# A hybrid decoder block on one Trainium2 core: sums of w_out's blocks made in DRAM by accumulating transfers instead of on GpSimd

## The chip, the core and the metric

The kernel runs on one core of a Trainium2 chip, as one program. The metric is device microseconds from one execution of the program; a time without further words is the median of several runs. The profile is one execution of its own, taken by the hardware profiler, with times in microseconds from the start of its span.

## The reference, cut to what matters

One decoder block on 1024 tokens of width 1024, with 16 meta tokens in front of them, so 1040 rows. All is float32.

```python
h = rmsnorm(x, norm_g)                       # 1040 x 1024
proj = h @ w_in                              # u_pool, z_pool, q, k, v, z_attn, f_logit, g_pool, g_attn
y_pool = causal_multiscale_pool(u_pool, pool_w, pool_scale) * silu(z_pool)
y_attn = forgetting_attention(q, k, v, log_f) * silu(z_attn)      # 8 heads of 64, causal
merged = sigmoid(g_pool) * (y_pool @ w_up_pool) + sigmoid(g_attn) * (y_attn @ w_up_attn)
out = rmsnorm(x + merged @ w_out, final_norm_g)   # w_out: 1024 x 1024
```

## The kernel before, in words

Every large product is made of three matmuls on high and low parts: an operand is rounded to float32r on ScalarE (the high part), and VectorE or GpSimd subtracts that from the operand (the low part).

The program has five stages. In the **first** (0 to about 56 us) the rows are read in nine tiles `xt` of 128 tokens (the ninth has 16). Of each tile ScalarE sums the squares (L184), VectorE adds the epsilon (L113), GpSimd raises to the power -0.5 (L114, `rstd`, through the helper `rstd_of`), VectorE scales the tile (L189), TensorE transposes it (L210, and L197 for the ninth tile), and ScalarE and VectorE make its high part `hh` (L212, L201) and low part `hl` (L213, L202). The list `todo` (L431 to L433) interleaves this with the projections of the first head pair: four token ranges times q, k and v. In the text the nine tiles are counted 0 to 8.

In the **second** stage (to about 503 us) the attention runs over 16 units (4 head pairs, 2 heads, 2 halves of the queries), in the loop at L682; the free time of TensorE is filled with the other projections, whose results are spilled to DRAM. In the **third** (to about 659 us) the pooling branch, the gates and the two up-projections follow, in the order of the list `steps`. The result `merged`, transposed, lies in eight tiles `G`; its four blocks of 512 by 512 are named "11" to "22" by `side`. The **fourth** (to about 736 us) is the product with `w_out` by seven products of blocks instead of eight (a Strassen-Winograd scheme): `prep` splits the operands of a product into high and low parts (`split_op`), `prod` runs 48 matmuls for each four output tiles, and `plus` and `arrive` add the results to the rows of x in `xr`. The **fifth** is the final norm and the stores.

The seven products need sums of blocks on both sides. On the side of `G` they are made by `s_first`, `s_second` and `s_third`. On the side of `w_out` they are made, in place in SBUF, by `t_first`, `t_second` and the second half of `s_third`, all on GpSimd, in pieces of 128x256, between 591 and 693 us. `w_load` brings `w_out` in as eight tiles `W` of 128 rows of 4 KB, one for each of eight up-projection steps.

What sets the order: TensorE's instructions run in the order in which the program is written. Those of the other engines, and the DMA issues of their queues (SP's above all), are put in order when the program is built, by a list scheduler that takes instructions as soon as it holds them to be ready, unless an `after` or `behind` ties them; each engine then runs its list in that order. The call `sums_of_w(i)` of the changed kernel stands in the loop over attention units, but its place in the code ties it to nothing.

Of the kernel before, what the change touches and what calls it, by code (L numbers as in the profile page):

```python
# [43 lines left out]
def r32(ap):  # L44
    return ap.bitcast(F32)
# [7 lines left out]
def tile_hybrid_block(ctx, tc, x, meta, norm_g, w_in, b_forget, pool_w, pool_scale,  # L53
                      w_up_pool, w_up_attn, w_out, final_g, out):
    nc = tc.nc
# [5 lines left out]
    wout = w_out[0].rearrange("(k p) n -> p k n", p=128)  # L61
# [6 lines left out]
    gp = ctx.enter_context(tc.tile_pool(name="gp", bufs=13))  # L68
    stg = ctx.enter_context(tc.tile_pool(name="stg", bufs=2))
    sm = ctx.enter_context(tc.tile_pool(name="sm", bufs=2))  # L70
    dr = ctx.enter_context(tc.tile_pool(name="dr", bufs=1, space=bass.MemoryType.DRAM))
# [28 lines left out]
    def after(ins, prev):  # L100
        tc.add_manual_dep(ins.ins, prev.ins.name,
                          mybir.DependencyInfo(mybir.DependencyClass.NoSync, mybir.DependencyReason.DATA),
                          reason="order")

    def behind(ins, prev):
        tc.add_manual_dep(ins.ins, prev.ins.name,
                          mybir.DependencyInfo(mybir.DependencyClass.Sync, mybir.DependencyReason.DATA),
                          reason="wait")
# [13 lines left out]
    def pool_tt(out, x, y, op):  # L122
        for c in range(0, out.shape[-1], 256):
            ins = nc.gpsimd.tensor_tensor(out[:, c:c + 256], x[:, c:c + 256], y[:, c:c + 256], op=op)  # L124
        return ins
# [142 lines left out]
    def v_piece(p, w, t0, t1):  # L268
        ps = yield from g_proj(w, t0, t1)
        nc.scalar.activation(VT[p][:, t0:t1], ps, AF.Copy)  # L270
# [59 lines left out]
    class Fill:  # L330
        def __init__(self):
            self.must, self.free, self.debt, self.now, self.cur, self.last = [], [], 0.0, 0, None, None
# [71 lines left out]
    def split_lo(raw, hi, pool, tag):  # L404
        lo = pool.tile([128, KO, 128], F32R, name="wlo", tag=tag)
        nc.gpsimd.tensor_tensor(lo, raw, r32(hi), op=ALU.subtract)
        return hi, lo
# [19 lines left out]
    wk = split_lo(rk, hk_, wp, "wl")  # L427
# [6 lines left out]
    for n, (kind, t0, t1) in enumerate(todo):  # L434
# [6 lines left out]
        else:  # L441
            g = v_piece(0, wv, t0, t1)
# [5 lines left out]
        i = {0: 2, 1: 3, 3: 4, 4: 5, 6: 6, 7: 7}.get(n)  # L448
# [7 lines left out]
        i = {1: 4, 2: 5, 4: 6, 5: 7, 6: 8}.get(n)  # L456
# [77 lines left out]
    for p in range(4):  # L534
        spill["y", p] = dr.tile([128, SEQ], F32, name=f"sp_y{p}")

    class Unit:
        def __init__(self, p, e, half):
            self.p, self.e, self.half = p, e, half
# [109 lines left out]
    def merged(a, c):  # L649
        out_ = []  # L650
        for lst in (a, c):
            tot = sum(s[0] for s in lst) or 1
            acc = 0.0
            for s in lst:
                out_.append(((acc + 0.5 * s[0]) / tot, s))
                acc += s[0]
        for _, (w, dve, pe, f) in sorted(out_, key=lambda t: t[0]):
            f()
            F.pull(max(0.0, PACE * dve - pe))
# [22 lines left out]
    for i, u in enumerate(units):  # L682
        nxt = units[i + 1] if i + 1 < 16 else None
        F.now = i
        if nxt is not None and nxt.p != u.p:
            F.until(f"q{nxt.p}", f"k{nxt.p}")
        merged(list(nxt.a_steps()) if nxt else [], list(u.c_steps()))
        for b in range(u.nb - LAG, u.nb):
            F.pull(LATENCY)
            u.av(b)  # L690
        if i == 1:
            after(nc.scalar.activation(pwh, pw, AF.Copy), exps[-1])
            nc.gpsimd.tensor_tensor(pwl, pw, r32(pwh), op=ALU.subtract)
        if nxt is not None:
            nxt.maxes()
        u.finish()
        if nxt is not None and nxt.p != u.p:
            F.until(f"v{nxt.p}")
            pair_fill(nxt.p + 1)
# [107 lines left out]
    G, gt, ya, muls = {}, {}, [], []  # L807
# [81 lines left out]
    hq = ctx.enter_context(tc.tile_pool(name="hq", bufs=8, side="right", reuse_waits="tile"))  # L889
# [4 lines left out]

    W = {}
    T_ = (slice(0, 512), slice(512, 1024))

    def w_load(k):
        W[k] = hq.tile([128, D], F32, name="W", tag="w")
        after(nc.sync.dma_start(W[k], wout[:, k, :]), muls[-1])  # L900

    def tt(out, x, y, op, eng):
        if eng is nc.gpsimd:
            pool_tt(out, x, y, op)
        else:
            eng.tensor_tensor(out, x, y, op=op)
# [5 lines left out]
    def pick(op_, k, n):  # L912
        return op_[n][k // 2][:, k % 2, :]

    def split_op(op_, k, src):
        h_ = pick(op_, k, 0)
        nc.scalar.activation(h_, src, AF.Copy)
        return nc.vector.tensor_tensor(pick(op_, k, 1), src, r32(h_), op=ALU.subtract)

    X3 = [gp.tile([128, 2, 512], F32, name="X3", tag="g") for _ in range(2)]  # L920
    Y3 = [gp.tile([128, 2, 512], F32, name="Y3", tag="g") for _ in range(2)]

    def side(d, k, blk):
        r, c = {"11": (0, 0), "12": (0, 1), "21": (1, 0), "22": (1, 1)}[blk]
        return d[k + 4 * r][:, T_[c]] if d is W else d[k + 4 * c][:, T_[r]]

    def t_first(k):
        tt(Y3[k // 2][:, k % 2, :], side(W, k, "22"), side(W, k, "12"), ALU.subtract, nc.gpsimd)
        tt(side(W, k, "12"), side(W, k, "12"), side(W, k, "11"), ALU.subtract, nc.gpsimd)

    def t_second(k):
        tt(side(W, k, "11"), side(W, k, "22"), side(W, k, "12"), ALU.subtract, nc.gpsimd)

    def s_first(k):
        tt(X3[k // 2][:, k % 2, :], side(G, k, "11"), side(G, k, "21"), ALU.subtract, nc.gpsimd)

    def s_second(k):
        tt(side(G, k, "21"), side(G, k, "21"), side(G, k, "22"), ALU.add, nc.vector)
        tt(side(G, k, "11"), side(G, k, "21"), side(G, k, "11"), ALU.subtract, nc.vector)

    def s_third(k, prev):
        for c in range(0, 512, 256):
            g12, g11 = [side(G, k, b)[:, c:c + 256] for b in ("12", "11")]
            ins = nc.gpsimd.tensor_tensor(g12, g12, g11, op=ALU.subtract)
            behind(ins, prev)
            w21, w11 = [side(W, k, b)[:, c:c + 256] for b in ("21", "11")]
            behind(nc.gpsimd.tensor_tensor(w21, w21, w11, op=ALU.subtract), prev)

    steps = [(0, 0), (1, 0), (2, 0), (3, 0), (0, 1)]
    for j in range(1, 8):  # L950
# [1 line left out]
    for n, s in enumerate(steps):  # L952
        for m, fn, d in ((n + 1, up_weights, ws), (n + 2, gate_row, rows_)):
            if m < len(steps) and steps[m] not in d:
                d[steps[m]] = fn(*steps[m])
        nxt = ws[steps[n + 1]][2] if n + 1 < len(steps) else None
        up(*s, ws.pop(s), rows_.pop(s), nxt)
        if n == 0:
            for p in range(4):
                attn_out(p)  # L960
        if 2 <= n < 10:
            w_load((0, 4, 1, 5, 2, 6, 3, 7)[n - 2])
            if n % 2:
                t_first((n - 2) // 2)
        j, a = s
        if a and j < 4:
            s_first(j)
        if s == (7, 0):
            opA, opB = operand("y"), operand("y")
        if a and j >= 4:  # L970
            if j < 6:
                for k in (2 * j - 8, 2 * j - 7):
                    split_op(opA, k, side(G, k, "11"))
                    split_op(opB, k, side(W, k, "11"))
                    t_second(k)
            if j == 5:
                s_second(0)
            if 4 < j < 7:
                s_second(j - 4)
# [18 lines left out]

    def plus(r, c0, ps):
        part = xr[r][:, c0:c0 + ps.shape[-1]]  # L1000
        return part, nc.vector.tensor_tensor(part, ps, part, op=ALU.add)

    def gain(r, c0, c1, eng):
        tt(xr[r][:, c0:c1], xr[r][:, c0:c1], fgb[:, c0:c1], ALU.mult, eng)
# [26 lines left out]
        after(nc.scalar.activation(o[:, b0:b1], xr[r][:, b0:b1], AF.Copy, scale=t), marks[-1][1])  # L1031
        nc.scalar.dma_start(o2[rr, b0:b1], o[:, b0:b1])

    srcs = [("11", "11"), ("12", "21"), ("11", "11"), ("21", "12"), (None, None), ("12", "22"), ("22", "21")]
    ops, lows = {0: (opA, opB)}, {}

    def prep(n):
        A_, B_ = operand("yh"[n % 2]), operand("yh"[n % 2])
        sa, sb = srcs[n]
        if n == 2:  # L1040
            s_second(3)
        for k in range(4):
            split_op(A_, k, side(G, k, sa) if sa else X3[k // 2][:, k % 2, :])
            lows[n] = split_op(B_, k, side(W, k, sb) if sb else Y3[k // 2][:, k % 2, :])
            if n == 3:
                s_third(k, lows[2])
        ops[n] = A_, B_

    lo_, hi_ = HALVES[0][0], HALVES[1][0]
    for n in range(7):  # L1050
        if n < 6:
            prep(n + 1)
        ps = ba if n in (0, 2, 4, 6) else bb_
# [56 lines left out]
```

## Time and profile before

| | |
|---|---|
| median of 3 runs | 744.41 us (744.18 to 745.41) |
| the profiled execution's own time | 743.96 us |
| its span | 742.2 us, so 1.76 us lie around the span |
| TensorE busy | 731.2 us, 99% |
| VectorE, ScalarE, GpSimd busy | 533.2, 377.0, 332.8 us |
| bytes moved by DMA | 75.35 MB |

A row of the timeline has the start, the duration, the engine, the line of the kernel, the operation, its output and inputs, a count where rows are merged, and in brackets how long the engine sat idle before it and whose event ended that. SPq is the queue on which SyncE issues transfers. A row of the windows has the stretch, its length, then for PE (TensorE), PEld (its weight load), DVE (VectorE), ACT (ScalarE) and POOL (GpSimd) the busy time and count, then TensorE's granted clock, the busy share of the DMA engines and GB/s. A row of the DMA table has the transfer, its queue, the count, the size of one and the median time from issue to landing.

### The profile page before, as it was taken

The page shows a single profiled execution, that of the slowest core. Times are in us where ns is not written, and L with a number is a line of the kernel's source. Part 1 is how long each engine was busy: PE and PEld are TensorE (multiplying, and loading weights), DVE is VectorE, ACT ScalarE, POOL GpSimd, SP SyncE. Part 2 cuts the span into 40 slices and gives each one's busy share as a digit, 9 for nine tenths or more (in the row PEclk, how much of TensorE's full clock was granted, in tenths as well). Part 3 has the DMA queues.
Part 4 walks back from the last instruction along what each step waited for, and adds up shares of the span by engine and source line. Part 5 has one row for each costly group of instructions (what it writes and reads, how often), then busy time and mean ns, then how long its engine had stood idle before and what let it go on. Part 6 is the DMA issues. An engine that isn't in the chain of part 4 may idle for free.

```text
span 742.2 us, 10619 instructions
## 1 busy us (share of the span) xinstructions
PE 731.2 (99%) x3686; PEld 622.7 (84%) x3686; DVE 533.2 (72%) x991; ACT 377.0 (51%) x736; POOL 332.8 (45%) x390
## 2 busy tenths in 40 slices
PE   8999999999999999999999999999999999999996
PEld 5997999988888898889988888888887888888885
DVE  5653577668779877688797687686288554997975
ACT  6662556446557545556563564452545322526445
POOL 4331235456426446345355383183348043606743
PEclk9999999999999999999999999999999999999998
DMA  9301132231312212222323223229375357360006
GB/s 301 88 15 43 29 86 86 62 98 23 95 48 60 80 50 90 78 53 55 94 66 86 80 80 92 72 81 309 95 201 212 142 200 240 116 224 1 1 0 227
DMA packets 76424, 75.35 MB, mean 102 GB/s; under 512 B 9665, under 2 KB 60865, under 8 KB 76370
## 3 DMA queue, kind: packets, MB, share of 16 engines
q1 hardware_dynamic: 74496, 69.95, 30.8%
q10 hardware_dynamic: 1874, 4.72, 1.7%
q8 instruction: 29, 0.48, 0.3%
q14 instruction: 25, 0.20, 0.1%
HBM read 55.58 MB, written 19.07 MB: 101 GB/s over the span
## 4 chain that ended last, share of the span: by engine, by line
PE 87%; DVE 5%; ACT 1%; issue 1%; POOLq 0%; POOL 0%; ACTq 0%
PE pj L152 65%; PE pj L995 8%; PE po L633 5%; PE ps L573 2%; PE ps L572 2%; PE pt L995 2%; PE pj L486 1%; DVE S L612 1%; DVE pl L617 1%; DVE ka L266 0%; PE pj L279 0%; DVE pt L603 0%; ACT S L581 0%; DVE mt L593 0%; ACT whi L140 0%
## 5 line engine op out<-in xcount | busy, mean ns | idle before, releaser
L124 POOL TENSOR_TENSOR wlo<-raw,whi 128x256 fp32r<-128x256 f32 x148 | 121.7, 852 | 192.5 <-ACT whi L140 96.1
L152 PE MATMUL pj<-hh,whi 128*128 128x512 f32 (+4 forms) x768 | 178.4, 360 | 0.6 <-ACT hh L201 0.3
L152 PE MATMUL pj<-hl,whi 128*128 128x512 f32 (+4 forms) x768 | 177.1, 359 | 0.0
L152 PE MATMUL pj<-hh,wlo 128*128 128x512 f32 (+4 forms) x768 | 174.4, 358 | 0.0
L152 PEld LDWEIGHTS pj<-hh,wlo 128*128 128x128 f32 x768 | 132.3, 188 | 18.1
L152 PEld LDWEIGHTS pj<-hh,whi 128*128 128x128 f32 x768 | 131.5, 188 | 18.7 <-ACT hh L201 0.5
L152 PEld LDWEIGHTS pj<-hl,whi 128*128 128x128 f32 x768 | 131.6, 188 | 17.7
L617 DVE TENSOR_TENSOR pl<-S,ph 128x512 fp32r<-128x512 f32 (+4 forms) x112 | 87.1, 792 | 19.3 <-ACT ph L616 18.8
L625 POOL TENSOR_TENSOR acc<-acc,S 128x272 f32<-128x272 f32 (+4 forms) x80 | 76.7, 958 | 11.2 <-ACT S L613 6.0
L581 ACT ACTIVATE S<-ps,negc 128x400 f32<-128x400 f32 (+2 forms) x96 | 49.3, 515 | 44.0 <-DVE S L579 35.7
L613 ACT ACTIVATE S<-S 128x512 f32<-128x512 f32 (+4 forms) x112 | 49.5, 478 | 33.7 <-DVE S L612 33.5
L616 ACT ACTIVATE ph<-S 128x512 fp32r<-128x512 f32 (+4 forms) x112 | 52.2, 480 | 15.8 <-PE po L633 14.4
L588 DVE TENSOR_TENSOR m<-m,S 128x272 f32<-128x272 f32 (+4 forms) x80 | 41.3, 517 | 23.8 <-ACT S L581 22.0
L140 ACT ACTIVATE whi<-raw 128x1024 fp32r<-128x1024 f32 x37 | 39.1, 1056 | 32.2 <-PE pj L152 27.8
L612 DVE TENSOR_TENSOR S<-S,pt 128x512 f32<-128x512 f32 (+4 forms) x112 | 51.9, 498 | 0.8
L836 DVE TENSOR_TENSOR rl<-pj,rl 128x512 f32<-128x512 f32 x32 | 22.0, 689 | 28.0 <-PE pj L152 28.0
L579 DVE SCALAR_TENSOR_TENSOR S<-ps,negc,mask 128x128 f32<-128x128 f32 (+2 forms) x72 | 23.7, 330 | 22.5 <-PE ps L573 22.3
L317 ACT ACTIVATE st<-pj 128x512 f32<-128x512 f32 x40 | 23.7, 593 | 28.1 <-PE pj L152 18.6
L633 PE MATMUL po<-pl,V 128*128 128x512 f32 (+4 forms) x112 | 37.6, 336 | 0.1
L573 PE MATMUL ps<-ql,ka 128*128 128x512 f32 (+4 forms) x112 | 37.5, 334 | 0.0
L572 PE MATMUL ps<-qa,ka 128*128 128x512 f32 (+4 forms) x112 | 36.0, 322 | 0.6 <-ACT S L581 0.5
L995 PE MATMUL pj<-opy 128*128 128x512 f32 (+1 forms) x168 | 36.3, 375 | 0.0
(187 smaller groups left out, 1134.2 us busy)
## 6 DMA issues: line engine op xcount, KB each, us to landing
raw<-in_w_in_dram SPq DMA_DIRECT2D x40, 512.0 KB, 3.9
sp_gp<-st SPq DMA_DIRECT2D x16, 256.0 KB, 2.0
sp_ga<-st SPq DMA_DIRECT2D x16, 256.0 KB, 2.0
rl<-sp_gp SPq DMA_DIRECT2D x8, 512.0 KB, 5.2
rl<-sp_ga SPq DMA_DIRECT2D x8, 512.0 KB, 4.5
W<-in_w_out_dram SPq DMA_DIRECT2D x8, 512.0 KB, 4.8
xr<-in_x_dram SPq DMA_DIRECT2D x8, 512.0 KB, 4.1
xt<-in_x_dram SPq DMA_DIRECT2D x7, 512.0 KB, 8.1
```

Source lines behind the costliest of these rows:

```text
L124: ins = nc.gpsimd.tensor_tensor(out[:, c:c + 256], x[:, c:c + 256], y[:, c:c + 256], op=op)
L152: nc.tensor.matmul(ps, a, b, start=(i == 0), stop=(i == len(seq) - 1))
L572: nc.tensor.matmul(ps[:kb, c0:], ka[:, k0:k0 + kb], qa[:, q0 + c0:q0 + 512], start=True, stop=False)
L573: nc.tensor.matmul(ps[:kb, c0:], ka[:, k0:k0 + kb], ql[:, q0 + c0:q0 + 512], start=False, stop=True)
L581: nc.scalar.activation(s[:kb, f0:], ps[:kb, f0:], AF.Identity, bias=nb_)
L612: nc.vector.tensor_tensor(s[:kb, c0:], s[:kb, c0:], self.pm[:kb, c0:], op=ALU.subtract)
L613: exps.append(nc.scalar.activation(s[:kb, c0:], s[:kb, c0:], AF.Exp))
L616: nc.scalar.activation(ph[:kb, c0:], s[:kb, c0:], AF.Copy)
L617: dves.append(nc.vector.tensor_tensor(pl[:kb, c0:], s[:kb, c0:], r32(ph[:kb, c0:]), op=ALU.subtract))
L625: nc.gpsimd.tensor_tensor(acc[:kb, c0:], acc[:kb, c0:], s[:kb, c0:], op=ALU.add)
L633: nc.tensor.matmul(self.po[:, c0:], v, r[:kb, c0:], start=(b == 0 and i == 0), stop=(b == self.nb - 1 and i == 1))
L995: nc.tensor.matmul(ps, pick(A_, k, p)[:, i * 128:(i + 1) * 128], pick(B_, k, q)[:, c0:c1], start=start and n == 0, stop=n == 11, skip_grou ...
```

## The change

The sums on the side of `w_out` are no longer made on GpSimd in SBUF. Four DRAM tensors of 512x512 (1 MB each) hold them: TD1 = W11 + W12, TD3 = W12 + W22, TD2 = TD3 + W11, TD4 = TD2 + W21. Each is first a plain copy (SP's queue), and then a transfer from GpSimd's queue adds a block of `w_out` to it at its destination (`accum_op`). The signs of the scheme are chosen anew so that all four are plain sums: the products that land in the right half are subtracted in `plus`, `split_op` makes a negated operand for product 2, and two combinations on the side of `G` change their sign. `w_load` now loads half a product's block (128x2x512, 512 KB) from `w_out` or from a TD; there are 14 of these loads instead of 8, and the last six are issued from `prep`. `t_first`, `t_second`, `Y3` and half of `s_third` are gone.

```diff
+    TD = {n: dr.tile([512, 512], F32, name=f"td{n}") for n in (1, 2, 3, 4)}
+    WB = {"11": w_out[0][:512, :512], "12": w_out[0][:512, 512:], "21": w_out[0][512:, :512], "22": w_out[0][512:, 512:]}
+
+    def sums_of_w(i):
+        if i == 2:
+            nc.sync.dma_start(TD[1], WB["11"])
+            nc.sync.dma_start(TD[3], WB["12"])
+        elif i == 4:
+            nc.gpsimd.dma_start(TD[1], WB["12"], accum_op=ALU.add)
+        elif i == 5:
+            nc.gpsimd.dma_start(TD[3], WB["22"], accum_op=ALU.add)
+        elif i == 7:
+            nc.sync.dma_start(TD[2], TD[3])
+        elif i == 8:
+            nc.gpsimd.dma_start(TD[2], WB["11"], accum_op=ALU.add)
+        elif i == 10:
+            nc.sync.dma_start(TD[4], TD[2])
+        elif i == 11:
+            nc.gpsimd.dma_start(TD[4], WB["21"], accum_op=ALU.add)
...
         u.finish()
+        sums_of_w(i)
...
-    def w_load(k):
-        W[k] = hq.tile([128, D], F32, name="W", tag="w")
-        after(nc.sync.dma_start(W[k], wout[:, k, :]), muls[-1])
+    WSRC = [WB["11"], WB["21"], TD[2], TD[1], TD[3], WB["22"], TD[4]]
+
+    def w_load(n, h):
+        W[n, h] = hq.tile([128, 2, 512], F32, name="W", tag="w")
+        return nc.sync.dma_start(W[n, h], WSRC[n].rearrange("(k p) c -> p k c", p=128)[:, 2 * h:2 * h + 2])
...
-    def split_op(op_, k, src):
+    def split_op(op_, k, src, neg=False):
         h_ = pick(op_, k, 0)
+        if neg:
+            nc.scalar.activation(h_, src, AF.Copy, scale=-1.0)
+            return nc.vector.scalar_tensor_tensor(pick(op_, k, 1), src, -1.0, r32(h_), op0=ALU.mult, op1=ALU.subtract)
...
-    def t_first(k):
-        tt(Y3[k // 2][:, k % 2, :], side(W, k, "22"), side(W, k, "12"), ALU.subtract, nc.gpsimd)
-        tt(side(W, k, "12"), side(W, k, "12"), side(W, k, "11"), ALU.subtract, nc.gpsimd)
-
-    def t_second(k):
-        tt(side(W, k, "11"), side(W, k, "22"), side(W, k, "12"), ALU.subtract, nc.gpsimd)
...
     def s_third(k, prev):
         for c in range(0, 512, 256):
             g12, g11 = [side(G, k, b)[:, c:c + 256] for b in ("12", "11")]
-            ins = nc.gpsimd.tensor_tensor(g12, g12, g11, op=ALU.subtract)
-            behind(ins, prev)
-            w21, w11 = [side(W, k, b)[:, c:c + 256] for b in ("21", "11")]
-            behind(nc.gpsimd.tensor_tensor(w21, w21, w11, op=ALU.subtract), prev)
+            behind(nc.gpsimd.tensor_tensor(g12, g11, g12, op=ALU.subtract), prev)
...
-        if 2 <= n < 10:
-            w_load((0, 4, 1, 5, 2, 6, 3, 7)[n - 2])
-            if n % 2:
-                t_first((n - 2) // 2)
+        if 4 <= n < 12:
+            after(w_load((n - 4) // 2, n % 2), muls[-1])
...
-        return part, nc.vector.tensor_tensor(part, ps, part, op=ALU.add)
+        if c0 < 512:
+            return part, nc.vector.tensor_tensor(part, ps, part, op=ALU.add)
+        return part, nc.vector.tensor_tensor(part, part, ps, op=ALU.subtract)
...
         ops[n] = A_, B_
+        if n < 4:
+            for h in range(2):
+                w_load(n + 3, h)
```

The change is a few lines of code, but it puts eight DMA issues into the lists of two queues. First stands GpSimd's list in the first stage of the kernel before, from the split of the first v weights on; `rstd` is the power of one tile, `ql` and `tri` are constants, and DMAHW and DMASW (in the next lists) are completions of transfers issued by SP or ScalarE, and by GpSimd.

```order
L406 TENSOR_TENSOR wlo<-raw,whi 128x1024 [waits DMAHW0_49,Activation_49]
L114 TENSOR_TENSOR rstd<-rstd,epsp 128x1 [waits DVE_49,Pool_49]
L480 MEMSET tri 128x256
L481 AFFINE_SELECT tri<-tri 128x128 [waits Pool_49]
L114 TENSOR_TENSOR rstd<-rstd,epsp 128x1 [waits DVE_49]
L223 MEMSET ql 64x1024 [waits Pool_49]
L223 MEMSET ql 64x1024
L114 TENSOR_TENSOR rstd<-rstd,epsp 128x1 [waits DVE_49,Pool_49]
L114 TENSOR_TENSOR rstd<-rstd,epsp 128x1 [waits DVE_49]
L114 TENSOR_TENSOR rstd<-rstd,epsp 16x1 [waits DVE_49]
```

In the changed kernel the same piece of GpSimd's list reads as follows, up to the last `rstd`. The names td_762, td_763, td_764 and td_765 are TD1, TD2, TD3 and TD4.

```order
L545 DMA td_762<-in_w_out_dram 512x512 [waits DMAHW4_49]
L114 TENSOR_TENSOR rstd<-rstd,epsp 128x1 [waits DVE_49,Pool_49]
L547 DMA td_764<-in_w_out_dram 512x512 [waits DMAHW5_49]
L480 MEMSET tri 128x256
L481 AFFINE_SELECT tri<-tri 128x128 [waits Pool_49]
L114 TENSOR_TENSOR rstd<-rstd,epsp 128x1 [waits DVE_49]
L223 MEMSET ql 64x1024 [waits Pool_49]
L223 MEMSET ql 64x1024
L551 DMA td_763<-in_w_out_dram 512x512 [waits DMAHW6_49]
L114 TENSOR_TENSOR rstd<-rstd,epsp 128x1 [waits DVE_49,Pool_49]
L555 DMA td_765<-in_w_out_dram 512x512 [waits DMAHW7_49]
L114 TENSOR_TENSOR rstd<-rstd,epsp 128x1 [waits DVE_49]
```

All four accumulating transfers have moved from the attention loop, where they are written, to among the `rstd` of tiles 4 to 8: one ahead of tile 4's, one ahead of tile 5's, one ahead of tile 6's, one ahead of those of tiles 7 and 8.

On SP's list the four plain copies stand behind the last small loads of the first stage (`psc`) and ahead of the weight loads of the second head pair (`raw`, L136). Before, the `raw` loads followed `psc` directly.

```order
L474 DMA psc<-in_pool_scale_dram 128x4x1 [waits DMAHW3_49]
L542 DMA td_762<-in_w_out_dram 512x512 [waits DMAHW4_49]
L543 DMA td_764<-in_w_out_dram 512x512 [waits DMAHW5_49]
L549 DMA td_763<-td_764 16x16384 [waits DMAHW6_49,DMASW1_49]
L553 DMA td_765<-td_763 16x16384 [waits DMAHW7_49,DMASW2_49]
L136 DMA raw<-in_w_in_dram 128x8x128 [waits DMAHW0_49,Activation_49,Pool_49]
```

The first two copies wait for nothing of the change; the third waits for the sum into TD3 (DMASW1), the fourth for the sum into TD2 (DMASW2). TensorE's list is the same in both kernels, and the lists of VectorE and ScalarE differ only in the stage of the seven products.

More of the change, by code (lines that the diff above doesn't have):

```diff
@@ L896, in tile_hybrid_block, with wk @@
     T_ = (slice(0, 512), slice(512, 1024))
-    def w_load(k):
-        W[k] = hq.tile([128, D], F32, name="W", tag="w")
-        after(nc.sync.dma_start(W[k], wout[:, k, :]), muls[-1])
+    WSRC = [WB["11"], WB["21"], TD[2], TD[1], TD[3], WB["22"], TD[4]]
+    def w_load(n, h):
+        W[n, h] = hq.tile([128, 2, 512], F32, name="W", tag="w")
+        return nc.sync.dma_start(W[n, h], WSRC[n].rearrange("(k p) c -> p k c", p=128)[:, 2 * h:2 * h + 2])
+    def wk(n, k):
+        return W[n, k // 2][:, k % 2, :]
     def tt(out, x, y, op, eng):
@@ L920, in tile_hybrid_block @@
     X3 = [gp.tile([128, 2, 512], F32, name="X3", tag="g") for _ in range(2)]
-    Y3 = [gp.tile([128, 2, 512], F32, name="Y3", tag="g") for _ in range(2)]
     def side(d, k, blk):
         r, c = {"11": (0, 0), "12": (0, 1), "21": (1, 0), "22": (1, 1)}[blk]
-        return d[k + 4 * r][:, T_[c]] if d is W else d[k + 4 * c][:, T_[r]]
-    def t_first(k):
-        tt(Y3[k // 2][:, k % 2, :], side(W, k, "22"), side(W, k, "12"), ALU.subtract, nc.gpsimd)
-        tt(side(W, k, "12"), side(W, k, "12"), side(W, k, "11"), ALU.subtract, nc.gpsimd)
-    def t_second(k):
-        tt(side(W, k, "11"), side(W, k, "22"), side(W, k, "12"), ALU.subtract, nc.gpsimd)
+        return d[k + 4 * c][:, T_[r]]
     def s_first(k):
@@ L937, in s_second @@
     def s_second(k):
-        tt(side(G, k, "21"), side(G, k, "21"), side(G, k, "22"), ALU.add, nc.vector)
-        tt(side(G, k, "11"), side(G, k, "21"), side(G, k, "11"), ALU.subtract, nc.vector)
+        tt(side(G, k, "21"), side(G, k, "22"), side(G, k, "21"), ALU.subtract, nc.vector)
+        tt(side(G, k, "11"), side(G, k, "21"), side(G, k, "11"), ALU.add, nc.vector)
     def s_third(k, prev):
@@ L973, in tile_hybrid_block @@
                     split_op(opA, k, side(G, k, "11"))
-                    split_op(opB, k, side(W, k, "11"))
-                    t_second(k)
+                    split_op(opB, k, wk(0, k))
             if j == 5:
@@ L1032, in store @@
         nc.scalar.dma_start(o2[rr, b0:b1], o[:, b0:b1])
-    srcs = [("11", "11"), ("12", "21"), ("11", "11"), ("21", "12"), (None, None), ("12", "22"), ("22", "21")]
+    srcs = ["11", "12", "11", "21", None, "12", "22"]
     ops, lows = {0: (opA, opB)}, {}
@@ L1038, in prep @@
         A_, B_ = operand("yh"[n % 2]), operand("yh"[n % 2])
-        sa, sb = srcs[n]
+        sa = srcs[n]
         if n == 2:
@@ L1042, in prep @@
         for k in range(4):
-            split_op(A_, k, side(G, k, sa) if sa else X3[k // 2][:, k % 2, :])
-            lows[n] = split_op(B_, k, side(W, k, sb) if sb else Y3[k // 2][:, k % 2, :])
+            split_op(A_, k, side(G, k, sa) if sa else X3[k // 2][:, k % 2, :], n == 2)
+            lows[n] = split_op(B_, k, wk(n, k))
             if n == 3:
```

## The prediction

> **What bounds the kernel now.** I read the page's totals first, then the busy time by stage, then what TensorE waited for, then the first 55 us engine by engine.
>
> ```profile
> PE 731.2 (99%) x3686; PEld 622.7 (84%) x3686; DVE 533.2 (72%) x991; ACT 377.0 (51%) x736; POOL 332.8 (45%) x390
> ```
>
> TensorE is busy for 731.2 of 742.2 us. By stages:
>
> ```profile
> 0.00:24.40 24.40, 21.67 (x119) 16.30 (x120) 13.69 (x32) 16.89 (x31) 11.60 (x20) 1.00 0.96 295
> 24.40:37.80 13.40, 13.40 (x117) 13.40 (x116) 8.97 (x19) 8.43 (x20) 3.23 (x5) 1.00 0.05 4
> 37.80:53.30 15.50, 14.67 (x120) 13.90 (x119) 9.07 (x21) 9.54 (x23) 3.92 (x6) 1.00 0.01 1
> 76.00:503.00 427.00, 426.09 (x2190) 372.66 (x2188) 329.58 (x691) 233.10 (x484) 205.70 (x233) 1.00 0.26 73
> 503.00:659.00 156.00, 156.00 (x673) 125.64 (x672) 100.28 (x116) 61.38 (x82) 64.71 (x64) 1.00 0.58 193
> 659.00:735.80 76.80, 76.69 (x349) 63.52 (x347) 62.19 (x89) 38.90 (x84) 38.17 (x55) 1.00 0.16 59
> 735.80:742.20 6.40, 0.00 (x0) 0.00 (x0) 1.76 (x3) 1.84 (x4) 0.74 (x2) 0.71 0.55 205
> ```
>
> In the up-projections (503 to 659 us) TensorE is busy for 156.00 of 156.00 us, and in the seven products (659 to 735.8) for 76.69 of 76.80. So whatever GpSimd does there on w_out, nobody on the path waits for it. The first stage is different. It is a tight chain through four engines; here are GpSimd's rows from the split of the v weights on:
>
> ```profile
> 19.53 2.40 POOL L406 TENSOR_TENSOR wlo<-raw,whi 128x1024 fp32r<-128x1024 f32 x1 [1.06 <-ACT whi L401]
> 23.46 0.55 POOL L114 TENSOR_TENSOR rstd<-rstd,epsp 128x1 f32<-128x1 f32 x1 [1.53 <-DVE rstd L113]
> 23.95 0.31 POOL L480 MEMSET tri<- 128x256 f32 x1
> 25.61 0.55 POOL L114 TENSOR_TENSOR rstd<-rstd,epsp 128x1 f32<-128x1 f32 x1 [0.97 <-DVE rstd L113]
> 33.73 0.56 POOL L114 TENSOR_TENSOR rstd<-rstd,epsp 128x1 f32<-128x1 f32 x1 [5.56 <-DVE rstd L113]
> 37.81 0.55 POOL L114 TENSOR_TENSOR rstd<-rstd,epsp 128x1 f32<-128x1 f32 x1 [3.53 <-DVE rstd L113]
> 42.02 0.54 POOL L114 TENSOR_TENSOR rstd<-rstd,epsp 16x1 f32<-16x1 f32 x1 [3.66 <-PE pt L210]
> 50.46 2.83 POOL L124 TENSOR_TENSOR wlo<-raw,whi 128x256 fp32r<-128x256 f32 x4 [7.91 <-ACT whi L140]
> ```
>
> The five rstd are the powers for tiles 4 to 8. The reader is to see two things. Each rstd starts as soon as its input is there. And the queue is in order: the memset of tri needs nothing, yet GpSimd sat idle for 1.53 us and ran it only behind the waiting rstd. What hangs on them, on VectorE and TensorE:
>
> ```profile
> 38.40 1.41 DVE L189 SCALAR_TENSOR_TENSOR xt<-xt,rstd,gb 128x512 f32<-128x512 f32 x2 [0.66 <-POOL rstd L114]
> 42.59 1.39 DVE L189 SCALAR_TENSOR_TENSOR xt<-xt,rstd,gb 16x512 f32<-16x512 f32 x2 [0.65 <-POOL rstd L114]
> 40.77 0.60 PE L210 MATMUL pn<-ident,xt 128*128 128x128 f32 x4
> 41.98 1.19 PE L152 MATMUL pj<-hh,whi 128*128 128x256 f32 x8
> 44.04 0.42 PE L197 MATMUL pt<-ident,xt 16*128 16x16 f32 x4 [0.22 <-DVE xt L189]
> ```
>
> Tile 7 is scaled by 39.81 and transposed at 40.77, less than 1 us of slack; the last transposes of tile 8 waited for its scaling, no slack at all. From there TensorE runs without a gap worth the name to 735.8 us, so a delay here is not won back.
>
> **The change part by part.** *Removed:* GpSimd's 32 pieces on w_out.
>
> ```profile
> L124 POOL TENSOR_TENSOR W<-W 128x256 f32<-128x256 f32 x16 | 15.5, 992 | 5.7 <-DVE opy L918 5.7
> L947 POOL TENSOR_TENSOR W<-W 128x256 f32<-128x256 f32 x8 | 7.2, 904 | 0.0
> L124 POOL TENSOR_TENSOR Y<-W 128x256 f32<-128x256 f32 x8 | 7.0, 892 | 36.5 <-PE pj L152 19.1 <-DMA W<-in_w_out_dram 17.4
> ```
>
> That is 15.5 + 7.2 + 7.0 = 29.7 us of GpSimd, all in the two stages in which TensorE has 0.11 us of idle time in total. Worth: 0 to 0.1 us; I take 0.
>
> *Altered in the products:* the negated low parts, the subtracting plus and the signs on G keep their counts, engines and shapes; four instructions merely become scalar_tensor_tensor. The medians (middle number, ns) for a 128x512 in the two forms:
>
> ```profile
> L189 DVE SCALAR_TENSOR_TENSOR xt<-xt,rstd,gb x18: 728/742/749, 7.2 to 43.3; 128x512 f32<-128x512 f32 x16, 16x512 f32<-16x512 f32 x2
> L918 DVE TENSOR_TENSOR opy<-G,opy x12: 680/692/1285, 635.7 to 718.9; 128x512 fp32r<-128x512 f32 x12
> ```
>
> 4 x 0.05 = 0.2 us of VectorE in all, under TensorE's 76.69: 0. The W loads become 14 of 512 KB, 3 MB more, in stages where the DMA engines are 58% and 16% busy. The last six are asked for three products, some 33 us, ahead; should SP hold one up, up to a product's prep could wait. I take 0.
>
> *Added, and moved by the scheduler:* four copies on SP and four accumulating transfers on GpSimd. By the lists they don't run during the attention; they run in the first stage. SP is free there:
>
> ```profile
> 23.11 1.29 SPq L474 DMA_DIRECT2D psc<-in_pool_scale_dram  x1
> 53.32 40.19 SPq L136 DMA_DIRECT2D raw<-in_w_in_dram  x4
> ```
>
> The two copies of w_out go out at 23.11 + 1.29 = 24.40 us, and SP has nothing due until 53.32. On GpSimd, rstd of tile 4 stands behind a transfer that waits for the copy into TD1; that of tile 5 behind one that waits for the copy into TD3; that of tile 6 behind one that waits for TD2's copy, hence for the finished sum TD3; and those of tiles 7 and 8 behind one that waits for TD4's copy, hence for the finished sum TD2. The last is the longest chain: copies, sum, copy, sum, copy, and GpSimd's issue of the fourth sum. All of VectorE's list behind L189 waits too, the evacuations of PSUM among it.
>
> No row shows a transfer from DRAM to DRAM, an accumulating one or an issue on GpSimd. The nearest rows:
>
> ```profile
> raw<-in_w_in_dram SPq DMA_DIRECT2D x40, 512.0 KB, 3.9
> sums<-sr SPq DMA_DIRECT2D x16, 8.0 KB, 1.4
> ```
>
> 8 KB take 1.4 us to land, 512 KB 3.9 us, so 1.4 us fixed and 2.5 us for each 512 KB. *A copy of 1 MB*: 1.4 + 5.0 = 6.4 us; the two at the start together 1.4 + 10.0 = 11.4 us. Low end: at the 295 GB/s of the first window, 3.6 us for 1 MB, so 5.0 alone and 8.5 for two. *An accumulating transfer*, from its issue to its landing: as low as a copy; as high as three passes of its bytes (read the source, read the destination, write), 1.4 + 15.0 = 16.4 us. I take two passes, 1.4 + 10.0 = 11.4, between the ends. *GpSimd's issue*: at least the 0.4 us that SP's shortest take; I take 2.4 us, the longest instruction GpSimd has here (L406); at most as long as the transfer itself. The sum:
>
> 24.4 + 11.4 (both copies) = 35.8; + 11.4 (sum TD3) = 47.2; + 6.4 (copy to TD2) = 53.6; + 11.4 (sum TD2) = 65.0; + 6.4 (copy to TD4) = 71.4; + 2.4 (issue) = 73.8 us, when rstd of tile 7 starts, instead of 37.81. That is **36.0 us** later. Tile 8 follows through VectorE as before (scaling at 42.59 against 38.40), so TensorE's transposes and everything behind them move by the same 36.0 us. The delays of tiles 4 to 6 lie inside this one. GpSimd's next work, the splits of the second pair's weights at 50.46 us, and SP's raw loads, free again at about 71.8 instead of waiting until 53.32, are needed by matmuls that moved by 36 us themselves: 0.
>
> With low ends for all: 24.4 + 8.5 + 4 x 5.0 + 0.4 = 53.3, 15.5 us later. With high ends for the sums and the issue: 35.8 + 16.4 + 6.4 + 16.4 + 6.4 + 16.4 = 97.8, 60.0 us later. Against the profiled execution's 743.96 us: 743.96 + 36.0 = **780.0 us**; the median of the runs, 744.41, is 0.45 us above it, which is left to the range.
>
> TensorE will idle several times for long. What an idle spell does to its clock, the end of the trace shows:
>
> ```profile
> 735.80:738.00 2.20, 0.00 (x0) 0.00 (x0) 1.32 (x3) 1.43 (x4) 0.74 (x2) 1.00 0.46 175
> 738.00:742.20 4.20, 0.00 (x0) 0.00 (x0) 0.44 (x1) 0.41 (x1) 0.00 (x0) 0.55 0.59 221
> ```
>
> 1.00 in the first 2.2 us without a matmul, 0.55 on average in the next 4.2. A slow restart costs nothing after the first gaps, which end in another wait. After the last, TensorE has about 2.4 us of work (40.77 to 41.98 + 1.19 = 43.17) until it needs tile 8, which comes 42.59 + 1.39 - 38.40 = 5.6 us after tile 7's scaling starts, so even at half speed it comes in time: 0. The Trainium skill, "TensorE: Matmul & The Clock Gate", Part 1, has the array at half rate after an idle window of about 3.4 us and until about 3.4 us of work have passed; taken in full that would be 1.7 us, 781.7 us instead of 780.0. The fall to 0.55 agrees with it; the restart after a gap no row here shows.
>
> **The rivals.** *The transfers are cheap* (759.5 us, 743.96 + 15.5): DRAM to DRAM at the rate of a busy stage, an accumulating one no dearer than a copy. For it: the DMA engines are 5% and 1% busy from 24.4 to 53.3 us. Against: at that rate 512 KB would land in 1.4 + 1.8 = 3.2 us, and the raw loads' median is 3.9. The page "DMA: Bandwidth & Descriptors" of the Trainium skill, section "Anatomy of one DMA — SWDGE (gpsimd) path", goes further this way, with about 2.0 us and the bytes by 436 GB/s for a transfer issued on GpSimd: 4.4 us for 1 MB, an estimate of about 757 us if it held for all of these.
>
> *GpSimd writes the transfer out piece by piece* (804.0 us, 743.96 + 60.0): the instruction lasts as long as the transfer, and the bytes pass three times. For it: 512 rows of 2 KB from three addresses each. Against: no row shows it. Each us on a sum costs 2 us, 3 if the issue lasts as long.
>
> *Not slower* (744.0 us): GpSimd hands the waiting transfer to its DMA queue and goes on with rstd, so nothing on the path waits; the 29.7 us of GpSimd saved then buy at most 0.1 us. It decides only if the wait isn't GpSimd's own, or if the whole chain fitted in 37.81 - 24.4 = 13.4 us, some 2 us for each of six steps, little above the fixed 1.4. Against it stands the memset of tri held behind a waiting rstd. The same time comes out if the transfers run in the attention after all, which the lists speak against.
>
> **How the numbers follow.** The forecast, 36 us of stall, 0.72; cheap transfers 0.10; slow ones 0.13; not slower 0.05. The range is 759 to 805: the cheap and the dear end, with not slower and the part beyond 805 left out. 0.2% (1.5 us) is about what a measurement of this kernel can tell from no change. Of the last rival I give 0.01 to faster by over 0.2% and 0.04 to no change; slower by over 0.2% is the rest, 0.95.
>
> **What would show it.** Right: TensorE waits for xt (L189) three or four times before about 76 us, the last one longest; VectorE's L189 waits for GpSimd's rstd; rstd of tile 7 starts right behind the fourth transfer's issue, at about 74; from there on every stage is as long as before (156.0 and 76.8 us for the last two). Wrong in size: the fourth issue comes much earlier or later; the landing times of the td transfers then say which price was off. Wrong in kind: rstd at 37.8 with the transfers still under way, or TensorE idle in the products, waiting for a W load.

## The result, and the profile after

The changed kernel takes 774.98 us (median, 774.76 to 776.78) against 744.58 us; the ratio is 1.0412, with a 95% interval of 1.0394 to 1.0430. That is 30.4 us slower; 780.0 us had been forecast, 759 to 805. The profiled execution took 774.76 us, with a span of 773.0 us, 30.8 us more than before.

The stages (columns as before: length, five engines, granted clock, DMA share, GB/s), the last two shifted by 31 us to where they now lie:

```profile
24.40:37.80 13.40, 7.30 (x45) 7.13 (x44) 3.75 (x8) 3.96 (x9) 6.02 (x8) 0.77 0.94 221
37.80:53.30 15.50, 8.55 (x71) 8.35 (x70) 4.38 (x9) 3.04 (x7) 1.66 (x2) 0.83 0.69 155
53.30:68.00 14.70, 6.58 (x33) 6.41 (x34) 2.15 (x6) 5.84 (x14) 1.67 (x2) 0.62 0.66 144
68.00:84.00 16.00, 14.98 (x87) 14.32 (x87) 7.88 (x20) 5.22 (x13) 2.75 (x5) 0.65 0.36 61
534.00:690.00 156.00, 156.00 (x672) 125.65 (x672) 95.77 (x117) 61.49 (x82) 42.37 (x40) 1.00 0.61 203
690.00:766.80 76.80, 76.57 (x348) 63.45 (x346) 59.10 (x88) 38.78 (x83) 29.13 (x47) 1.00 0.22 80
```

The up-projections and the products take 156.0 and 76.8 us, to the tenth what they took before, with 31.4 us less of GpSimd in them (42.37 + 29.13 against 64.71 + 38.17) and 32 instructions fewer. The loss lies before 84 us. From 24.4 to 68 us TensorE is busy for about half of the time, and to 84 us its granted clock is down to 0.62 to 0.83 on average, where it had been 1.00. GpSimd's list in this stretch, to be read against its rows of before:

```profile
30.34 1.28 POOL L545 DMA_DIRECT2D td<-in_w_out_dram  x1 [7.98 <-DMA td<-in_w_out_dram]
31.26 0.98 POOL L114 TENSOR_TENSOR rstd<-rstd,epsp 128x1 f32<-128x1 f32 x1
33.13 1.08 POOL L547 DMA_DIRECT2D td<-in_w_out_dram  x1 [0.89 <-DMA td<-in_w_out_dram]
34.88 0.56 POOL L114 TENSOR_TENSOR rstd<-rstd,epsp 128x1 f32<-128x1 f32 x1
50.64 1.06 POOL L551 DMA_DIRECT2D td<-in_w_out_dram  x1 [13.19 <-DMA td<-td]
51.35 0.96 POOL L114 TENSOR_TENSOR rstd<-rstd,epsp 128x1 f32<-128x1 f32 x1
65.24 1.08 POOL L555 DMA_DIRECT2D td<-in_w_out_dram  x1 [12.93 <-DMA td<-td]
65.94 0.96 POOL L114 TENSOR_TENSOR rstd<-rstd,epsp 128x1 f32<-128x1 f32 x1
70.57 0.54 POOL L114 TENSOR_TENSOR rstd<-rstd,epsp 16x1 f32<-16x1 f32 x1 [3.66 <-DVE rstd L113]
```

Each DMA row is an issue that waited for a copy (in brackets: 13.19 us idle, ended by the landing of td<-td), and behind it follows the rstd that stands there in the list: at once in three cases, behind the two short instructions on `tri` in the case of 33.13. The rstd of tile 7 starts at 65.94 us instead of 37.81. SP's copies, and three of TensorE's four longest waits (total, times, longest):

```profile
23.02 0.78 SPq L542 DMA_DIRECT2D td<-in_w_out_dram  x1
23.84 1.77 SPq L543 DMA_DIRECT2D td<-in_w_out_dram  x1
44.94 0.47 SPq L549 DMA_DIRECT2D td<-td  x1
59.69 0.47 SPq L553 DMA_DIRECT2D td<-td  x1
```

```profile
PE pn L210 <- issue: 14.2, 2, 8.1
PE pt L210 <- DVE xt L189: 7.1, 2, 7.0
PE pt L210 <- DVE hl L213: 1.0, 1, 1.0
```

SP issues the third copy at 44.94, when the sum into TD3 has landed, and the fourth at 59.69, when the sum into TD2 has. TensorE waits three times for 6 to 8 us ahead of transposes (L210). Two of the waits stand under "issue", but the chain of waits that ended last names what was behind them; in this stretch it runs through the transfers:

```profile
23.84 8.99 DMA td<-in_w_out_dram
37.45 13.18 issue
50.64 9.03 DMA td<-in_w_out_dram
59.69 5.20 DMA td<-td
65.24 1.08 POOL td L555
```

The 13.18 us that the chain can't assign lie within the sum into TD3 (33.13 to 44.94) and the copy out of it (44.94 to 50.64), by the rows of SP and GpSimd above.

### The profile page after: what moved, and what is told of

It reads as the page before. It is cut to its first block, busy times and chain, and to the rows that moved or that the text cites. A ratio compares the mean times of both kernels' runs of the same rounds, so it can differ in the third digit from the quotient of the medians.

```text
span 773.0 us, 10618 instructions
## 1 busy us (share of the span) xinstructions
PE 741.7 (96%) x3686; PEld 633.3 (82%) x3686; DVE 525.1 (68%) x991; ACT 377.3 (49%) x736; POOL 306.7 (40%) x362
## 3 DMA queue, kind: packets, MB, share of 16 engines
q0 software_dynamic: 2112, 4.19, 3.3%
## 4 chain that ended last, share of the span: by engine, by line
PE 90%; issue 3%; DMA 3%; DVE 2%; POOL 1%; SPq 0%; ACT 0%; POOLq 0%; ACTq 0%; DVEq 0%
PE pj L152 68%; PE pj L1009 8%; PE po L653 5%; PE ps L593 3%; DMA td<-in_w_out_dram 2%; PE ps L592 2%; PE pt L1009 2%; PE pj L486 1%; DMA td<-td 1%; PE pj L279 0%; PE pt L210 0%; POOL rstd L114 0%; DVE xt L189 0%; DVE S L632 0%; POOL ql L223 0%
## 5 line engine op out<-in xcount | busy, mean ns | idle before, releaser
L152 PE MATMUL pj<-hh,whi 128*128 128x512 f32 (+4 forms) x768 | 182.5, 367 | 0.2 <-DVE V L285 0.2
L152 PE MATMUL pj<-hl,whi 128*128 128x512 f32 (+4 forms) x768 | 179.8, 364 | 0.0
L152 PEld LDWEIGHTS pj<-hh,whi 128*128 128x128 f32 x768 | 135.6, 196 | 17.9 <-PE pj L279 0.4
L152 PEld LDWEIGHTS pj<-hl,whi 128*128 128x128 f32 x768 | 134.3, 193 | 17.7
```

The costliest lines, as they stand in the source:

```text
L152: nc.tensor.matmul(ps, a, b, start=(i == 0), stop=(i == len(seq) - 1))
```

## The experiments

The theory: the whole loss is GpSimd's list in the first stage, held by waits ahead of its DMA issues, plus TensorE's restart at a low clock. Its rivals: the traffic, the altered products, the issue itself. For comparing executions one number helps, the span behind the start of tile 7's rstd, here called the rest: 742.2 - 37.81 = 704.4 us before, 773.0 - 65.94 = 707.1 us in the changed kernel. In the runs below without a stall (tied, no transfers, the same places without a wait) it was 704.6, 704.0 and 704.3 us.

**Tied to the attention.** Each of the eight transfers gets a place behind its unit's last subtraction of a low part on VectorE (`dves[-1]`):

```diff
-            nc.gpsimd.dma_start(TD[1], WB["12"], accum_op=ALU.add)
+            after(nc.gpsimd.dma_start(TD[1], WB["12"], accum_op=ALU.add), dves[-1])
```

> The eight transfers are tied to the attention unit behind which they are written, so they leave the first stage; nothing else changes. Theory (the loss is GpSimd's queue held in the first stage): rstd of tile 7 starts at about 37.8 us again and the time is 744.5 us, within 1 us. Rival (the 12 MB that these transfers and the longer W loads move, or the altered products, carry part of it): 747 us or more, with TensorE waiting in the attention or in the products.

744.74 us, ratio 1.0003 (0.9995 to 1.0012). The transfers are issued from 165.3 to 396.9 us, and GpSimd never waits for one. So the transfers, the longer loads and the altered products together cost nothing that can be measured, and the 29.7 us of GpSimd work saved bring nothing either. Two rows of GpSimd's:

```profile
39.05 0.55 POOL L114 TENSOR_TENSOR rstd<-rstd,epsp 128x1 f32<-128x1 f32 x1 [3.53 <-DVE rstd L113]
43.26 0.54 POOL L114 TENSOR_TENSOR rstd<-rstd,epsp 16x1 f32<-16x1 f32 x1 [3.66 <-PE pt L210]
```

They wait for VectorE and TensorE again, for as long as in the kernel before, and the rest is 743.6 - 39.05 = 704.6 us.

**Only the transfers.** The kernel before, with `TD`, `sums_of_w` and its call added:

```diff
         u.finish()
+        sums_of_w(i)
```

> The kernel before with the eight transfers added as in the change, and its own sums on GpSimd kept; nobody reads the four DRAM sums. Theory: the whole loss, 775 us, within 1.5 us. Rival (the altered products carry part of it): below 773 us.

777.08 us, ratio 1.0438 (1.0424 to 1.0452): the whole loss, without any of the altered products. It is 0.6 us outside what was expected. Its profile shows where that comes from: the second copy let GpSimd go at 35.25 us instead of 33.13, and tile 7's rstd started at 68.58; the rest is 775.6 - 68.58 = 707.0 us, as in the changed kernel.

**No transfers.** The other half, the altered products with plain blocks in place of the sums:

```diff
-        sums_of_w(i)
...
-    WSRC = [WB["11"], WB["21"], TD[2], TD[1], TD[3], WB["22"], TD[4]]
+    WSRC = [WB["11"], WB["21"], WB["12"], WB["12"], WB["12"], WB["22"], WB["21"]]
```

> The changed kernel without the eight transfers; the loads that would read a sum read a plain block of w_out of the same size, so four of seven products are of other operands. Theory: 744.5 us, within 0.7 us: 29.7 us less GpSimd work buys nothing, 3 MB more loads cost nothing. Rival (a W load that waits holds up a product): 746 us or more, with TensorE waiting for a split of W.

744.51 us, ratio 0.9999 (0.9990 to 1.0007). The two parts are apart: the transfers carry all of the loss, the products none and no gain.

**The same places, no wait.** GpSimd's four transfers are written into the first stage, so that its list has them ahead of the same four rstd. They copy plainly and wait for nothing; SP's four copies are left out:

```diff
+        t = {1: (1, "12"), 2: (3, "22"), 4: (2, "11"), 5: (4, "21")}.get(n)
+        if t is not None:
+            nc.gpsimd.dma_start(TD[t[0]], WB[t[1]])
         if i is not None:
             norm_scale(xts[i], ntok(i), norm_stat(xts[i], ntok(i)))
```

> GpSimd's four transfers stay at the same places among the rstd, but copy plainly and depend on nothing; SP's four copies are left out, so the DRAM tensors hold blocks and not sums. Theory (the wait ahead of the issue costs, not the issue): each issue holds GpSimd for about 0.7 us, so rstd of tiles 7 and 8 come about 1 us late: 744.5 to 747 us, 745.5 taken. Rival (issuing a transfer on GpSimd, or its traffic, holds the queue for long by itself): over 750 us.

744.72 us, ratio 1.0004 (0.9995 to 1.0012). Three issues with the rstd behind them, and the windows over them:

```profile
23.58 0.89 POOL L464 DMA_DIRECT2D td<-in_w_out_dram  x1
24.56 0.56 POOL L116 TENSOR_TENSOR rstd<-rstd,epsp 128x1 f32<-128x1 f32 x1
29.24 0.68 POOL L464 DMA_DIRECT2D td<-in_w_out_dram  x1
34.81 0.56 POOL L116 TENSOR_TENSOR rstd<-rstd,epsp 128x1 f32<-128x1 f32 x1 [4.88 <-DVE rstd L115]
35.34 0.68 POOL L464 DMA_DIRECT2D td<-in_w_out_dram  x1
38.91 0.56 POOL L116 TENSOR_TENSOR rstd<-rstd,epsp 128x1 f32<-128x1 f32 x1 [2.89 <-DVE rstd L115]
```

```profile
24.40:37.80 13.40, 13.40 (x117) 13.40 (x117) 9.18 (x19) 7.83 (x19) 6.21 (x11) 1.00 0.88 256
37.80:53.30 15.50, 14.64 (x119) 13.85 (x119) 8.61 (x21) 9.65 (x24) 2.81 (x5) 1.00 0.15 54
```

An issue takes 0.7 to 0.9 us and costs TensorE nothing; 3.4 of the 4 MB go through the DMA engines in the first window, at 256 GB/s, while TensorE stays busy for 13.40 of 13.40 us. The place and this traffic alone cost nothing. In the changed kernel the same rows have the wait in front; besides, they add instead of copying, and SP's 4 MB of copies run too. The run "Plain instead of accumulating" below keeps the waits and the copies without the add and still takes 768.48 us, so it is the wait ahead of the issue.

**Two sums tied.** Only TD2 and TD4 get a place in the attention, with `after` as above; TD1 and TD3 stay.

> Only the chained sums (TD2 and TD4, two copies and two accumulating transfers) are tied to their attention units; TD1 and TD3 stay in the first stage. Theory (the delays of the tiles lie one inside the other, and the last rstd held decides): rstd of tile 5 comes at about 35 instead of 25.6 us, those of tiles 6 to 8 wait for nothing new, so about 9.5 us remain, with a slow restart of TensorE up to 2 us more: 754 us, 752 to 757. Rival (each held rstd adds its own stall): half of the loss or more, 760 us.

755.35 us, ratio 1.0150 (1.0133 to 1.0167). In its profile tile 5's rstd starts at 35.41 us, and tile 7's at 46.63, 8.8 us late, with nothing left to wait for but VectorE:

```profile
33.67 1.07 POOL L547 DMA_DIRECT2D td<-in_w_out_dram  x1 [0.59 <-DMA td<-in_w_out_dram]
35.41 0.55 POOL L114 TENSOR_TENSOR rstd<-rstd,epsp 128x1 f32<-128x1 f32 x1
42.55 0.56 POOL L114 TENSOR_TENSOR rstd<-rstd,epsp 128x1 f32<-128x1 f32 x1 [4.57 <-DVE rstd L113]
46.63 0.55 POOL L114 TENSOR_TENSOR rstd<-rstd,epsp 128x1 f32<-128x1 f32 x1 [3.53 <-DVE rstd L113]
```

So the delays do lie one inside the other, and the last rstd held decides. This execution took less than the median (752.32 us; the other three, 754.77 to 756.25, have no profile), with a span of 750.6 us, and its rest is 704.0 us.

**TensorE kept at work in the last stall.** 34 matmuls into an unused PSUM tile ahead of tile 7's transposes:

```diff
+        if n == 7:
+            keep = psG.tile([128, 4, 128], F32, name="pn")
+            for _ in range(34):
+                nc.tensor.matmul(keep, onesr, onesr[:, None, :].to_broadcast([128, 4, 128]), start=True, stop=True)
```

> The changed kernel with 34 matmuls of 128x512 into an unused PSUM tile ahead of tile 7's transposes, about 8 us of work in the last stall. Theory (about 2.7 us of the loss are matmuls at the low clock after the last stall): rstd of tile 7 at the same time as before, the matmuls behind it at full rate: 772.3 us, 2 to 3.5 us less than the changed kernel's 775.0. Rival (the shift behind the last stall comes from VectorE's chain or from buffers and not from the clock): 775 us or more.

776.16 us, ratio 1.0422 (1.0406 to 1.0437): by the time alone the rival, since nothing was gained over the 774.98 of another set of runs. But tile 7's rstd didn't come at the same time; it started at 69.26 us instead of 65.94, because the two first copies landed 3.2 us later, and the rest was 774.3 - 69.26 = 705.0 us, 2.1 less than in the changed kernel. So both kernels were run once more beside each other. First the changed kernel, without an edit:

> The changed kernel once more, so that the next one has it beside it on the same chip. Both theories: 775 to 777 us; the start of tile 7's rstd moves by 2 to 3 us between executions with the landing of the two first copies.

775.94 us (774.45 to 777.85), ratio 1.0429 (1.0414 to 1.0445); rest 776.1 - 69.01 = 707.1 us. Then the one with the 34 matmuls:

> The kernel with 34 matmuls ahead of tile 7's transposes once more, now beside the changed kernel. Theory (low clock behind the last stall): the median 1.5 to 2.5 us under that of the changed kernel, and the span behind tile 7's rstd 705 us against 707. Rival (no effect of the clock): the medians agree within 0.7 us.

774.12 us (772.98 to 777.52), ratio 1.0417 (1.0397 to 1.0436); rest 771.2 - 66.57 = 704.6 us. The medians differ by 1.8 us as expected, but their ranges overlap, and by them alone it would stay open. The rests, 705.0 and 704.6 against 707.1, 707.0 and 707.1, don't overlap; the two runs below that are stalled and not kept at work have 706.4 and 707.5. The matmuls behind tile 7's transposes, first in the kernel before, then in the changed kernel (first profile), then with the 34 matmuls (second run):

```profile
44.38 1.20 PE L152 MATMUL pj<-hl,whi 128*128 128x256 f32 x8
48.08 1.16 PE L152 MATMUL pj<-hl,whi 128*128 128x272 f32 x8
```

```profile
67.79 1.08 PE L210 MATMUL pn<-ident,xt 128*128 128x128 f32 x4 [8.12 <-issue]
71.09 2.06 PE L152 MATMUL pj<-hh,whi 128*128 128x256 f32 x8
74.03 2.08 PE L152 MATMUL pj<-hl,whi 128*128 128x256 f32 x8
77.61 1.94 PE L152 MATMUL pj<-hh,whi 128*128 128x272 f32 x8
79.39 1.17 PE L152 MATMUL pj<-hl,whi 128*128 128x272 f32 x8
```

```profile
58.96 7.89 PE L452 MATMUL pn<-onesr 128*128 128x512 f32 x34
68.42 0.63 PE L210 MATMUL pn<-ident,xt 128*128 128x128 f32 x4 [1.56 <-issue]
71.53 2.05 PE L152 MATMUL pj<-hh,whi 128*128 128x256 f32 x8
74.37 1.22 PE L152 MATMUL pj<-hl,whi 128*128 128x256 f32 x8
77.36 1.16 PE L152 MATMUL pj<-hl,whi 128*128 128x272 f32 x8
```

Eight matmuls that take 1.1 to 1.2 us take 1.9 to 2.1 us from 71.09 to about 79.3 us in the changed kernel. With TensorE kept at work the first eight (71.53) are still slow, and from 74.37 on they are back at 1.1 to 1.2: the granted clock was 0.50 for 3.4 us, from 70.8 to 74.2, where it was 0.50 for 17.1 us in the changed kernel, from 62.3 to 79.3. One place in the list shows it without the rest of the span: the last row of each block starts 10.27 us behind tile 7's rstd before (48.08 - 37.81), 13.45 in the changed kernel (79.39 - 65.94) and 10.79 with the 34 matmuls (77.36 - 66.57). By the rests, keeping TensorE at work is worth 2.0 to 2.5 us.

**Plain instead of accumulating.** GpSimd's four transfers with the same places and waits:

```diff
-            nc.gpsimd.dma_start(TD[1], WB["12"], accum_op=ALU.add)
+            nc.gpsimd.dma_start(TD[1], WB["12"])
```

> The four transfers of GpSimd keep their places, waits and bytes but don't add, so the DRAM tensors hold plain blocks. Theory (adding makes a transfer two passes): a transfer alone lands in 5.7 us like SP's copies instead of 9.0, the one that shares the engines with another in 8.5 instead of 11.8, together 6.6 us less: 768.4 us. Rival (a transfer issued on GpSimd is that slow with or without the add): 775 us.

768.48 us, ratio 1.0325 (1.0309 to 1.0340), and 6.5 us less than with the add. That it meets the expected 768.4 to the tenth is luck: in the profile tile 7's rstd came 5.7 us earlier (60.27) and not 6.6, and the rest was 706.4 us and not 707.1. From issue to the copy that waited for it:

```profile
33.31 0.69 POOL L547 DMA_DIRECT2D td<-in_w_out_dram  x1 [1.96 <-DMA td<-in_w_out_dram]
47.68 0.68 POOL L551 DMA_DIRECT2D td<-in_w_out_dram  x1 [10.44 <-DMA td<-td]
41.41 0.47 SPq L549 DMA_DIRECT2D td<-td  x1
53.84 0.47 SPq L553 DMA_DIRECT2D td<-td  x1
```

8.1 us (41.41 - 33.31) where the sum took 11.8, and 6.2 us (53.84 - 47.68) where the sum, alone on the engines, took 9.0.

**Half of the rows.** The accumulating transfers cover `[:256]` of both sides:

```diff
-            nc.gpsimd.dma_start(TD[1], WB["12"], accum_op=ALU.add)
+            nc.gpsimd.dma_start(TD[1][:256], WB["12"][:256], accum_op=ALU.add)
```

> The four accumulating transfers cover only the first 256 rows, half of the bytes; the copies are whole. The lower halves of the DRAM tensors are therefore not sums. Theory (an accumulating transfer costs 1.4 us and the rest by the byte): 9.0 becomes 5.2 us and 11.8 becomes 6.6, 9.0 us less: 766 us. Rival (most of it is a fixed cost of such a transfer): 773 us or more.

769.46 us, ratio 1.0341 (1.0326 to 1.0357), between the two theories. The sum into TD2 was issued at 49.70 us and its copy at 55.83: 6.1 us for 512 KB against 9.0 for 1 MB. A line through these two points has 2.9 us for 512 KB and 3.2 us fixed, more than the 1.4 us of the theory; no third size was run. The profiled execution is the longest of the four (771.19 us; the others took 769.4 to 769.5): the second of the first copies landed late in it (GpSimd's issue at 35.96 us, 2.8 us later than in the changed kernel's).

## Why the prediction was right, point by point

**The place and the mechanism** held: SP's and GpSimd's lists as built, not the place in the code, told where the transfers run; GpSimd was held ahead of its issues; the four delays lie one inside the other; nothing behind the first stage changed in length. The runs with the transfers alone (777.08), without them (744.51), tied (744.74), without the wait (744.72), and with the wait but without the add (768.48) leave no other cause of this size. *Not slower* fell: GpSimd does not hand the wait on.

**The sum** was 36.0 us for tile 7's rstd; it came 65.94 - 37.81 = 28.1 us late. Term by term, predicted and measured:

| step | predicted, us | measured, us | from the rows of |
|---|---|---|---|
| first copy issued at | 24.4 | 23.0 | SP L542 |
| both copies | 11.4 | 10.1 | GpSimd L547 less SP L542 |
| sum TD3 | 11.4 | 11.8 | SP L549 less GpSimd L547 |
| copy to TD2 | 6.4 | 5.7 | GpSimd L551 less SP L549 |
| sum TD2 | 11.4 | 9.0 | SP L553 less GpSimd L551 |
| copy to TD4 | 6.4 | 5.6 | GpSimd L555 less SP L553 |
| issue of the fourth sum | 2.4 | 0.7 | rstd less GpSimd L555 |

The terms are 7.9 us too dear together, and two of them carry half of it: the issue 1.7 us, the sum into TD2 2.4. The rest is 1.4 us in the start of the first copy (SP was done with `psc` earlier than in the profile of before), 1.3 in the first two copies and 1.5 in the other two, against 0.4 too few in the sum into TD3. The issue of an accumulating transfer lets the next instruction start after 0.7 us, near the low end (0.4), not the middle I took. And the two sums are not alike: the one into TD3 still shares the DMA engines with the one into TD1, issued 2.8 us before it (GpSimd's queue moved 2.05 MB from 33 to 45 us, nearly both sums); the one into TD2 runs alone and takes 9.0 us. Two passes by the rate of the plain loads (11.4) were thus right for the wrong reason in the first case and too many in the second. GpSimd's plain transfer takes 6.2 us alone, so the add costs 2.9 us more, about half of a plain one.

**The clock** was put at 0, and that step failed. I had reckoned that half speed would only touch the 2.4 us of work ahead of tile 8's transposes, and that TensorE would still come to them in time. It came late: tile 8 was scaled 5.6 us after tile 7's scaling began (71.14 + 1.39 - 66.94), as reckoned, but TensorE reached its transposes only after 6.1 us (73.07 - 66.94). The work started 0.85 us after that scaling began (67.79) and took 5.3 us instead of 2.4, 1.0 of them a wait for `hl` (the last of the waits above). In rows, VectorE's scaling of tiles 7 and 8 in the changed kernel, and TensorE's transposes of tile 8:

```profile
66.94 1.41 DVE L189 SCALAR_TENSOR_TENSOR xt<-xt,rstd,gb 128x512 f32<-128x512 f32 x2 [11.19 <-POOL rstd L114]
71.14 1.39 DVE L189 SCALAR_TENSOR_TENSOR xt<-xt,rstd,gb 16x512 f32<-16x512 f32 x2 [0.66 <-POOL rstd L114]
73.07 1.03 PE L197 MATMUL pt<-ident,xt 16*128 16x16 f32 x8
```

So the matmuls behind tile 8's transposes began 8.1 us behind tile 7's rstd (74.03) instead of 6.6 (44.38). From there TensorE is the bound again, and the clock stayed at 0.50 to 79.3 us. At the next row shown the delay has grown to 3.2 us (13.45 against 10.27).

By the rests it is 707.1 - 704.4 = 2.7 us, of which the 34 matmuls took back 2.0 to 2.5. The sum left out a second term of 0.4 us: tile 7's rstd itself takes 0.96 us, directly behind an accumulating issue, instead of 0.55, so that its scaling starts 1.00 us behind its start (66.94 - 65.94) instead of 0.59 (38.40 - 37.81).

The Trainium skill's "TensorE: Matmul & The Clock Gate", Part 1, with half rate until about 3.4 us of work have passed, was nearer with the estimate of 1.7 us. Behind the first stall the trace agrees with it: matmuls run without a break from 34.71 us, and from 38.27 at full rate, 3.6 us. Behind the last it took longer: 8.2 us from the first matmuls (71.09) and 5.3 us from those behind tile 8's transposes (74.03) to the full clock at 79.3 us. Why stays open. The small transposes that lie between (73.07 to 74.03 us) can't be the whole answer: with the 34 matmuls the same ones lie between too, and the clock was full again 2.6 us behind the first of the slow matmuls (71.53 to 74.17).

**28.1 + 2.7 = 30.8 us**, the difference of the spans. The forecast was 5.0 us too high: 7.9 us too much in the chain, 2.7 us left out with the clock and the slower rstd, 0.2 in what lies between the executions and the medians. That the two errors point opposite ways, so that the time came nearer than the chain, is luck.

**The rivals.** *Cheap transfers*: the copies came near it (5.7 and 5.6 against its 5.0), the sums not (9.0 and more). By the Trainium skill's "DMA: Bandwidth & Descriptors", section "Anatomy of one DMA — SWDGE (gpsimd) path", a transfer of this size from GpSimd would take 4.4 us, an estimate. Here, from DRAM to DRAM, it takes 6.2 us plain and 9.0 us adding, so the measurement decides against it. *Piece by piece*: the instruction ends after 1.1 us, long before the transfer.

## What to carry to other kernels

A transfer issued from GpSimd waited on GpSimd here: what stood behind it in the list waited too, however little it had to do with it. Where a scheduler orders the lists, read them before believing that a call stands where it was written, and tie such a call to work near it; here one `after` per transfer was worth 30 us. And work taken off an engine that nobody waits for was worth nothing that could be measured here: 29.7 us of GpSimd, for a ratio of 0.9999 (0.9990 to 1.0007).

## What the runs showed of the hardware that I had not expected

- An accumulating transfer of 1 MB from DRAM to DRAM took 9.0 us alone and 6.1 us for half of the rows; the plain one from the same queue took 6.2 us. The queue moved 2112 packets for four sums against 1088 for four plain transfers.
- An rstd directly behind an accumulating issue took 0.96 to 0.99 us instead of 0.55 (0.88 to 0.91 behind one of half of the rows); behind a plain one 0.56 to 0.59.
- The landing of the two first copies varied by some 3 us between executions (GpSimd's second issue at 33.13 to 36.30 us in the profiles that have the same list), and the times of the profiled executions go with it: 33.13, 35.25 and 35.72 us with 774.76, 777.30 and 777.85 us.
- The granted clock changed in steps. In the first 90 us of the eight traces with a stall, the stretches of one clock value between two changes lasted 3.41, 6.83, 10.24, 13.65 or 17.07 us, all multiples of 3.41. The last one at 0.50 lasted 17.07 us in the three profiles of the changed list and of the transfers alone, 13.65 in the runs with plain and with half transfers, and 3.41 in both with the 34 matmuls. So the price of a slow restart isn't one number; what decides it was not tested.
